# Norm roots and spreads one or two tiles sooner, and two projection pieces between a head's loads and the head

## The chip, the cores and the metric

The kernel runs on one core of one Trainium2 chip. The metric is the device time of one execution in microseconds (us): the median of several runs. A profile is one execution recorded by the hardware profiler.

## The reference

The program is a two-layer backbone over 512 latent tokens and 256 context tokens, model width 1024, all in float32. In each layer, with the same weights for both kinds of token:

- a half-step feed-forward block: the input is normalised by its root mean square, scaled and shifted by a condition ("modulated"), multiplied up to two times 2816 columns, gated with silu, multiplied down, and added to the stream;
- one mixing step: norm and modulation again, one projection to queries, keys and values, split into group A (8 heads, 2-D neighbourhood attention) and group B (8 heads, windowed attention with shared keys, rotary angles and a sink), then an output projection;
- a second half-step feed-forward block.

The norm is what the change is about:

```python
def rms_norm(x, g):
    xf = x.astype(jnp.float32)
    y = xf * lax.rsqrt(jnp.mean(xf * xf, axis=-1, keepdims=True) + NORM_EPS)
    return (y * g.astype(jnp.float32)).astype(x.dtype)

def modulate(h, shift, scale):
    return h * (1 + scale) + shift
```

In the second layer the context has no queries and no second feed-forward block. The output is the latent stream.

## The kernel before

**Numbers and layout.** Activations are kept transposed: 128 partitions by 8 slices d of the model width by 768 token columns (512 latent, 256 context). Every matrix product is done as three products of split operands: each float32 operand becomes a high part (cast on ACT) and a low part (difference on DVE), and PE adds high x high, high x low and low x high (lines 559 to 561 and 930 to 932). The activations' parts are `xh` and `xl`; the weights' are `whi` and `wlo`, made 512 columns at a time by `halves` (148 and 149).

**Token streams.** Most stages run over three streams of 256 columns, `THIRDS`: latent first half, latent second half, context. The last stage of a block goes stream by stream: for each, its tiles of the down projection (or of the output projection, `out_final`), a residual on DVE (807), a square on ACT (475) and a sum of squares on DVE (476). When a stream's tiles are done, `background` starts the next norm of that stream as a Python generator, which moves on by one step with each later call of `tick`.

**The norm as a background job.** `norm` waits `root - 1` ticks, then issues `rstd`: products with a column of ones on PE (505), a scale on DVE (507) and the power -1/2 on POOL (508). At tick `spread` it issues the transposes on PE that spread the result over all partitions into a PSUM bank (514), and then, for eight slices d, the modulation: a multiplication on DVE (520), `xh` on ACT (524), `xl` on DVE (525). Each slice from the third on is to be issued behind the `xl` of two slices earlier. The products of `rstd` and the transposes are to be issued behind the last product traced so far. The pairs (root, spread) come from one table, by kind and stream:

```python
TICKS = {"ffn": [(3, 6), (3, 6), (5, 8)], "mix": [(3, 6), (3, 4), (2, 3)], "lat": [(2, 3), (3, 6)]}
```

"ffn" is a norm in front of a feed-forward block with three streams (twice in the program), "mix" one in front of the mixing step (twice), "lat" one in front of the last block, with two streams (once). `tick` is called after each tile of the last stage, after each two slices in the plain products of the next feed-forward block, and after each piece of the projection. So tick 6 of the first stream falls in the third stream's tiles. The first norm of the program, at its start, doesn't use the table.

**The mixing step.** The projection is cut into nine units of 256 columns (`UNITS`), each into pieces of 128 tokens: 24 products on PE, then a copy to `raw` on ACT (942, two buffers), squares, a reduction, the root on POOL, and for group B the rotation on DVE (960 to 973); the rows go to a scratch in DRAM by SP's queue (981 to 986). The units of group B come first; from then on a piece has a single PSUM bank, tag "mm". Then come 16 heads, B first. `head` loads a pair's query rows (`load_pair`, 1026), values (`load_v`) and keys (`load_k`, through `load_keys`, 994) from the scratch, transposes them on PE (1010) and splits them (1034, 1035, 1070, 1071); `qn` and `kn`, which the loads fill, have one buffer each. `scores` multiplies (1148, 1149). Between the heads `fill` places the other pieces, and then the output projection, by shares of their total.

**Who sets the order.** The program order gives priorities; the order on each engine is fixed when the program is built, by a scheduler that has its own clock (`schedule_with_timeline_sim=True`). An instruction that the scheduler holds ready can go ahead of one that is traced before it. `issue_after` adds an order on one engine that the scheduler must keep. On the chip each engine then runs its own list in order.

Of the kernel before, what the change touches and what calls it, by code (L numbers as in the profile page):

```python
# [10 lines left out]
F32 = mybir.dt.float32  # L11
# [6 lines left out]
P = 128  # L18
D = 1024
KD = 8  # L20
S = 512
C = 256
T = S + C
# [19 lines left out]
SQ, SK, SV = 0, 1024, 2304  # L43
# [123 lines left out]

TICKS = {"ffn": [(3, 6), (3, 6), (5, 8)], "mix": [(3, 6), (3, 4), (2, 3)], "lat": [(2, 3), (3, 6)]}  # L170

FULL = [(0, 0, S), (1, S, T)]
LAT = [(0, 0, S)]
# [4 lines left out]
class Kern:  # L178
# [132 lines left out]
    def background(self, then, i, n, b, s0, s1):  # L311

        kind = "lat" if n == 2 else "mix" if then[1] == 1 else "ffn"
        self.bg.append((self.norm(*then, b, s0, s1, *TICKS[kind][i]), s0))

# [496 lines left out]
    def mixing(self, l, last):  # L812
        nc, ws = self.nc, self.ws
        base = self.at["in", l]
        streams = LAT if last else FULL
        n = streams[-1][2]
        with ExitStack() as c2:
            self.pp = self.open(c2, "ps_m", space=bass.MemoryType.PSUM, reuse_waits="tile")
            self.fp = self.ap = self.open(c2, "mix", reuse_waits="tile")
            self.banks = ("t", TB)  # L820
            self.x = self.ap.tile([P, KD, T], F32, tag="x", name="x")
            self.next_slot, self.wide = 0, -1
            self.jobs, self.held, self.free = [], [], False
            ws.after(base)
            pieces = [(u, t) for u in range(9) for t in range(4 if (last and UNITS[u][0][0] == "q") else 6)]

            def piece():
                u, t = pieces.pop(0)
                if t == 0:
                    self.unit = ws.get(base + u)  # L830
                    ws.after(base + u + 1)
                self.flush(t * P)
                self.project(l, u, t)
                self.tick()
                if not pieces:

                    self.free = True
                    for f in self.held:
                        f()
                    self.held = []  # L840

            with ExitStack() as c3:
                self.rp = self.open(c3, "rope", reuse_waits="tile")
                self.rope_tables(l)
                self.early = True
                while pieces and UNITS[pieces[0][0]][0][-1] == "B":
                    piece()
                self.early = False
            bp = self.open(c2, "bias", reuse_waits="tile")

            self.bias = bp.tile([P, 7, 256], F32, name="bias")
            self.bmask = bp.tile([P, 896], F32, name="bmask")
            nc.sync.dma_start(self.bmask, self.a["bmask"])
            nc.gpsimd.memset(self.bias[:, 3], 0.0)
            outs = [(u, d, z) for u in range(4) for d in (2 * u, 2 * u + 1) for z in streams]

            def out():
                u, d, (b, s0, s1) = outs.pop(0)
                if d % 2 == 0 and s0 == 0:
                    i = self.at["out", l] + u  # L860
                    self.wout = ws.get(i)
                    ws.after(i + 1)
                self.out_b(l, self.wout, d, b, s0, s1)

            cost = lambda: 1.0 if pieces else (outs[0][2][2] - outs[0][2][1]) / S
            total = len(pieces) + sum((z[2][2] - z[2][1]) / S for z in outs)
            state = [0.0]

            def fill(share):
                while (pieces or outs) and state[0] < total * share:  # L870
                    state[0] += cost()
                    piece() if pieces else out()

            nj = 2 if last else 3
            order = list(range(8, 16)) + list(range(8))
            nxt = None
            for i, hh in enumerate(order):
                loaded = nxt or self.head(l, last, hh)
                for j in range(nj):
                    if j == nj - 1 and i < 15:  # L880
                        h2 = order[i + 1]
                        if h2 % 4 == 0 and h2 < 8:

                            while pieces and UNITS[pieces[0][0]][1] % 512 <= 64 * h2:
                                state[0] += 1.0
                                piece()
                        nxt = self.head(l, last, h2)
                    self.push(self.scores(l, hh % 8, hh < 8, ((0, 1), (2, 3), (4, 5))[j], loaded))
                    n = i * nj + j
                    fill((n + 1 + LEAD) / (16 * nj))  # L890
            while self.jobs:
                self.values(*self.jobs.pop(0))
            fill(2.0)
# [118 lines left out]

    def load_pair(self, l, last, pair, A):

        nc, ap, scr = self.nc, self.ap, self.scr
        nq = S if last else T
        qn = ap.tile([P, 6, P], F32, tag="qn", name="qn", bufs=1)
        cs = slice(SQ + pair * P, SQ + pair * P + P)
        if A:
            lat = scr[0:S, cs].rearrange("(r w) c -> r w c", w=64)  # L1020
            for t in range(4):
                nc.sync.dma_start(qn[:, t, :], lat[:, t * 16:t * 16 + 16, :])
            if not last:
                nc.sync.dma_start(qn[:, 4:6], scr[S:T, cs].rearrange("(t p) c -> p t c", p=P))
        else:
            nc.sync.dma_start(qn[:, :nq // P], scr[:nq, cs].rearrange("(t p) c -> p t c", p=P))
        q = [ap.tile([P, T], F32R, tag=f"q{e}", name=f"q{e}", bufs=QB) for e in range(2)]
        for ts in ((0, 1, 2, 3), (4, 5))[:1 if last else 2]:
            src = self.transposed([qn[:, t, :] for t in ts])
            cols = slice(ts[0] * P, ts[-1] * P + P)  # L1030
            for e in range(2):
                own, oth = (slice(0, 64), slice(64, 128)) if e == 0 else (slice(64, 128), slice(0, 64))
                sc = self.gq8[own, l, 0:1] if A else 1.0
                nc.scalar.activation(out=q[e][own, cols], in_=src[own], func=AF.Copy, scale=sc)
                nc.vector.scalar_tensor_tensor(out=q[e][oth, cols], in0=src[own], scalar=sc,
                                               in1=q[e][own, cols].bitcast(F32), op0=ALU.mult, op1=ALU.subtract)
        return q

    def load_v(self, pair, A):

# [17 lines left out]
    def load_k(self, l, A, head, kcol):  # L1058

        nc, ap = self.nc, self.ap  # L1060
        kn = ap.tile([P, 6, P], F32, tag="kn", name="kn", bufs=1)
        self.load_keys(kn, kcol, P, A)
        order = VSLOT if A else range(6)
        kh = ap.tile([P, T], F32R, tag="kh", name="kh", bufs=KB)
        kl = ap.tile([P, T], F32R, tag="kl", name="kl", bufs=KB)
        sc = self.gcol[:, l, 1:2] if A else 1.0
        for ts in ((0, 1, 2, 3), (4, 5)):
            src = self.transposed([kn[:, order[t]] for t in ts])
            cols = slice(ts[0] * P, ts[-1] * P + P)
            nc.scalar.activation(out=kh[:, cols], in_=src, func=AF.Copy, scale=sc)  # L1070
            nc.vector.scalar_tensor_tensor(out=kl[:, cols], in0=src, scalar=sc, in1=kh[:, cols].bitcast(F32),
                                           op0=ALU.mult, op1=ALU.subtract)
        return kh, kl

    def block(self, b, A, head):

# [263 lines left out]
```

## Time and profile before

| what | value |
|---|---|
| median of the runs | 2666.98 us (2657.66 to 2667.18) |
| the profiled execution | 2666.63 us |
| its span, first to last instruction | 2664.5 us |
| mean granted clock of TensorE | 0.992 |
| PE busy | 2589.8 us, 97% |
| DVE busy | 2087.8 us, 78% |
| ACT busy | 1284.1 us, 48% |
| POOL busy | 142.0 us, 5% |

PE is the engine for matrix products, PEld its weight loads, DVE the vector engine, ACT the scalar engine, POOL GpSimd, SP the queue that issues the transfers. A line such as "PE mm L932 <- DVE xl L525: 6.1, 5, 2.0" means that PE stood idle in front of products of line 932 until DVE had written `xl` on line 525, for 6.1 us in all, in 5 places, the longest 2.0 us. A row of a timeline has the start and the length in us, the engine, the line, the operation, out<-in, the shape, the count, and in brackets the idle time in front and what ended it. Names with numbers are merged, so `b`, `t`, `mm` and `sc` are PSUM banks, `st` the small tile of the roots (and, on the lines 935 to 986, a row buffer), `x` a slice of the stream.

### The profile page before, as it was taken

The numbers are of one execution on the slowest core, as the hardware profiler recorded it, in microseconds if no ns is written. First come the engines' busy times: TensorE is split into PE (matmuls) and PEld (weight loads), VectorE is DVE, ScalarE is ACT, GpSimd is POOL, SyncE is SP. The second block draws the span as 40 slices with busy tenths as digits, with TensorE's granted clock in tenths as the row PEclk, the third lists the DMA queues.
The fourth block names the chain that finished last, engine by engine and source line by source line (L and its number), as shares of the span: only waits on it lengthen the run. The fifth ranks groups of instructions, "written<-read, shape, count | busy, mean of one in ns | idle before, by whom it ended". The sixth has DMA issues, their size and how long they took to land. (4 is left out here: it accounts for less than half of the span.)

```text
span 2664.5 us, 47447 instructions
## 1 busy us (share of the span) xinstructions
PE 2589.8 (97%) x17186; PEld 2462.1 (92%) x17186; DVE 2087.8 (78%) x4190; ACT 1284.1 (48%) x2666; POOL 142.0 (5%) x231
## 2 busy tenths in 40 slices
PE   7999999989999999999999999999988999899999
PEld 5999999989999899999999999999988998899998
DVE  7998898677889788777776887686766778777776
ACT  6343343445777653343334533432444677554543
POOL 0000000024111000000000000000003111000000
PEclk9999999999999999999999999999999999999999
DMA  8666647335235536455444366466344336355553
GB/s 321 223 206 204 221 157 223 114 119 152 88 100 163 175 92 214 140 176 185 145 156 133 112 222 211 141 217 209 105 149 135 103 107 183 96 175 166 165 163 116
DMA packets 305866, 431.66 MB, mean 162 GB/s; under 512 B 31408, under 2 KB 177200, under 8 KB 304304
## 3 DMA queue, kind: packets, MB, share of 16 engines
q1 hardware_dynamic: 305632, 428.64, 51.2%
q8 instruction: 135, 2.21, 0.3%
q14 instruction: 99, 0.81, 0.1%
HBM read 343.33 MB, written 88.34 MB: 162 GB/s over the span
## 5 line engine op out<-in xcount | busy, mean ns | idle before, releaser
L148 ACT CAST whi<-wraw 128x512 fp32r<-128x512 f32 (+1 forms) x632 | 381.6, 609 | 698.7 <-PE b L560 595.5
L149 DVE TENSOR_TENSOR wlo<-wraw,whi 128x512 fp32r<-128x512 f32 (+1 forms) x632 | 417.2, 673 | 65.6 <-ACT whi L148 46.1
L561 PE MATMUL b<-xh,wlo 128*128 128x384 f32 (+2 forms) x1472 | 453.9, 313 | 2.6 <-DVE wlo L149 2.6
L560 PE MATMUL b<-hl,whi 128*128 128x512 f32 (+1 forms) x1292 | 432.6, 337 | 0.0
L560 PE MATMUL b<-xl,whi 128*128 128x384 f32 (+2 forms) x1344 | 423.4, 316 | 6.8 <-DVE xl L525 6.6
L561 PE MATMUL b<-hh,wlo 128*128 128x512 f32 (+1 forms) x1292 | 428.8, 336 | 0.0
L559 PE MATMUL b<-xh,whi 128*128 128x384 f32 (+2 forms) x1344 | 418.2, 316 | 2.9 <-ACT xh L524 2.0
L559 PE MATMUL b<-hh,whi 128*128 128x512 f32 (+1 forms) x1292 | 414.5, 337 | 0.0
L560 PE MATMUL b<-x,whi 128*128 128x384 f32 (+1 forms) x1216 | 390.8, 322 | 0.0
L559 PE MATMUL b<-sh,whi 128*128 128x384 f32 (+1 forms) x1216 | 389.8, 323 | 0.4
L561 PE MATMUL b<-sh,wlo 128*128 128x384 f32 (+1 forms) x1216 | 384.0, 322 | 0.5 <-DVE wlo L149 0.5
L461 DVE CUSTOM_DVE_ANT_0 junk<-adaw,sc,bada 128x1024 bf16<-128x1024 f32 x224 | 286.5, 1279 | 15.8 <-DMA adaw<-in_w_ada 15.2
L561 PEld LDWEIGHTS b<-xh,wlo 128*128 128x128 f32 x1472 | 277.0, 189 | 7.5 <-DVE wlo L149 4.3
L148 ACT CAST whi<-wt 128x512 fp32r<-128x512 f32 x228 | 141.8, 622 | 272.6 <-PE b L560 246.7
L560 PEld LDWEIGHTS b<-hl,whi 128*128 128x128 f32 x1292 | 244.7, 189 | 24.9
L561 PEld LDWEIGHTS b<-hh,wlo 128*128 128x128 f32 x1292 | 244.3, 189 | 25.0
L560 PEld LDWEIGHTS b<-xl,whi 128*128 128x128 f32 x1344 | 254.3, 189 | 12.1 <-DVE xl L525 8.1
L559 PEld LDWEIGHTS b<-hh,whi 128*128 128x128 f32 x1292 | 241.1, 189 | 26.0
L559 PEld LDWEIGHTS b<-xh,whi 128*128 128x128 f32 x1344 | 251.8, 189 | 7.3 <-ACT xh L524 2.4
L932 PE MATMUL mm<-whi,xl 128*128 128x256 f32 x800 | 227.9, 287 | 12.1 <-DVE xl L525 12.1
L930 PE MATMUL mm<-whi,xh 128*128 128x256 f32 x800 | 232.1, 292 | 5.2 <-ACT raw L942 4.9
L559 PEld LDWEIGHTS b<-sh,whi 128*128 128x128 f32 x1216 | 228.7, 188 | 3.6 <-ACT whi L148 2.2
(166 smaller groups left out, 4982.9 us busy)
## 6 DMA issues: line engine op xcount, KB each, us to landing
wraw<-in_w_up SPq DMA_DIRECT2D x352, 256.0 KB
adaw<-in_w_ada SPq DMA_DIRECT2D x129, 512.0 KB
wraw<-in_w_down SPq DMA_DIRECT2D x160, 256.0 KB
xsp<-x SPq DMA_DIRECT2D x140, 256.0 KB
xsp<-x SPq DMA_DIRECT2D x184, 128.0 KB
xl<-xsp SPq DMA_DIRECT2D x80, 256.0 KB
xh<-xsp SPq DMA_DIRECT2D x80, 256.0 KB
wraw<-in_w_in SPq DMA_DIRECT2D x72, 256.0 KB
```

What stands on the lines that cost most here:

```text
L148: k.nc.scalar.copy(hi[:, :w], raw[:, :w])
L149: k.nc.vector.tensor_tensor(out=lo[:, :w], in0=raw[:, :w], in1=hi[:, :w].bitcast(F32), op=ALU.subtract)
L461: nc.vector.tensor_tensor_reduce(out=junk, in0=w, in1=self.sc[:, cond, :], scale=1.0, scalar=self.bada[:, l, n:n + 1], op0=ALU.mult, op1=A ...
L559: mm(o, wh, h, start=first, stop=False, skip_group_check=more)
L560: mm(o, wh, l, start=False, stop=False, skip_group_check=more)
L561: self.product = mm(o, wl, h, start=False, stop=last, skip_group_check=more)
L930: nc.tensor.matmul(o, self.xh[:, k, ts], wh, start=k == 0, stop=False)
L932: self.product = nc.tensor.matmul(o, self.xl[:, k, ts], wh, start=False, stop=k == KD - 1)
```

## The change

Three things:

- In `TICKS`, the first two streams of "ffn" and "mix" get the root at tick 2 and the spread at tick 4; the third stream of "mix" gets them at ticks 1 and 2. "lat" and the third stream of "ffn" stay.
- The loads of query rows and of keys are taken out of `load_pair` and `load_k` into functions of their own, `rows_of` and `keys_of`, which first look in the list `asked`.
- In `mixing`, ahead of the heads, the loads of the first head (pair 4 and the keys at SK + 1024) are put into `asked`, and two pieces of the projection are traced behind them; the first head then takes the two tiles from the list. The two pieces are counted in `state`, so `fill` places two fewer behind the first scores.

```diff
--- before.py
+++ after.py
@@ -167,7 +167,7 @@
 
 
 
-TICKS = {"ffn": [(3, 6), (3, 6), (5, 8)], "mix": [(3, 6), (3, 4), (2, 3)], "lat": [(2, 3), (3, 6)]}
+TICKS = {"ffn": [(2, 4), (2, 4), (5, 8)], "mix": [(2, 4), (2, 4), (1, 2)], "lat": [(2, 3), (3, 6)]}
 
 FULL = [(0, 0, S), (1, S, T)]
 LAT = [(0, 0, S)]
@@ -820,7 +820,7 @@
             self.banks = ("t", TB)
             self.x = self.ap.tile([P, KD, T], F32, tag="x", name="x")
             self.next_slot, self.wide = 0, -1
-            self.jobs, self.held, self.free = [], [], False
+            self.jobs, self.held, self.free, self.asked = [], [], False, []
             ws.after(base)
             pieces = [(u, t) for u in range(9) for t in range(4 if (last and UNITS[u][0][0] == "q") else 6)]
 
@@ -873,6 +873,12 @@
 
             nj = 2 if last else 3
             order = list(range(8, 16)) + list(range(8))
+
+            asked = [self.rows_of(l, last, 4, False), self.keys_of(False, SK + 1024)]
+            self.asked = asked
+            for _ in range(2):
+                state[0] += 1.0
+                piece()
             nxt = None
             for i, hh in enumerate(order):
                 loaded = nxt or self.head(l, last, hh)
@@ -1012,18 +1018,8 @@
 
     def load_pair(self, l, last, pair, A):
 
-        nc, ap, scr = self.nc, self.ap, self.scr
-        nq = S if last else T
-        qn = ap.tile([P, 6, P], F32, tag="qn", name="qn", bufs=1)
-        cs = slice(SQ + pair * P, SQ + pair * P + P)
-        if A:
-            lat = scr[0:S, cs].rearrange("(r w) c -> r w c", w=64)
-            for t in range(4):
-                nc.sync.dma_start(qn[:, t, :], lat[:, t * 16:t * 16 + 16, :])
-            if not last:
-                nc.sync.dma_start(qn[:, 4:6], scr[S:T, cs].rearrange("(t p) c -> p t c", p=P))
-        else:
-            nc.sync.dma_start(qn[:, :nq // P], scr[:nq, cs].rearrange("(t p) c -> p t c", p=P))
+        nc, ap = self.nc, self.ap
+        qn = self.rows_of(l, last, pair, A)
         q = [ap.tile([P, T], F32R, tag=f"q{e}", name=f"q{e}", bufs=QB) for e in range(2)]
         for ts in ((0, 1, 2, 3), (4, 5))[:1 if last else 2]:
             src = self.transposed([qn[:, t, :] for t in ts])
@@ -1035,6 +1031,24 @@
                 nc.vector.scalar_tensor_tensor(out=q[e][oth, cols], in0=src[own], scalar=sc,
                                                in1=q[e][own, cols].bitcast(F32), op0=ALU.mult, op1=ALU.subtract)
         return q
+
+    def rows_of(self, l, last, pair, A):
+
+        if self.asked:
+            return self.asked.pop(0)
+        nc, scr = self.nc, self.scr
+        nq = S if last else T
+        qn = self.ap.tile([P, 6, P], F32, tag="qn", name="qn", bufs=1)
+        cs = slice(SQ + pair * P, SQ + pair * P + P)
+        if A:
+            lat = scr[0:S, cs].rearrange("(r w) c -> r w c", w=64)
+            for t in range(4):
+                nc.sync.dma_start(qn[:, t, :], lat[:, t * 16:t * 16 + 16, :])
+            if not last:
+                nc.sync.dma_start(qn[:, 4:6], scr[S:T, cs].rearrange("(t p) c -> p t c", p=P))
+        else:
+            nc.sync.dma_start(qn[:, :nq // P], scr[:nq, cs].rearrange("(t p) c -> p t c", p=P))
+        return qn
 
     def load_v(self, pair, A):
 
@@ -1058,8 +1072,7 @@
     def load_k(self, l, A, head, kcol):
 
         nc, ap = self.nc, self.ap
-        kn = ap.tile([P, 6, P], F32, tag="kn", name="kn", bufs=1)
-        self.load_keys(kn, kcol, P, A)
+        kn = self.keys_of(A, kcol)
         order = VSLOT if A else range(6)
         kh = ap.tile([P, T], F32R, tag="kh", name="kh", bufs=KB)
         kl = ap.tile([P, T], F32R, tag="kl", name="kl", bufs=KB)
@@ -1071,6 +1084,14 @@
             nc.vector.scalar_tensor_tensor(out=kl[:, cols], in0=src, scalar=sc, in1=kh[:, cols].bitcast(F32),
                                            op0=ALU.mult, op1=ALU.subtract)
         return kh, kl
+
+    def keys_of(self, A, kcol):
+
+        if self.asked:
+            return self.asked.pop(0)
+        kn = self.ap.tile([P, 6, P], F32, tag="kn", name="kn", bufs=1)
+        self.load_keys(kn, kcol, P, A)
+        return kn
 
     def block(self, b, A, head):
```

## The prediction

> **What bounds the kernel now.** I read the page's engine line first, then PE's waits over the whole span, then the same view around each norm, then the stretches. The columns of a wait: total us, times, longest us.
>
> ```profile
> span 2664.5 us, 47447 instructions
> ...
> PE 2589.8 (97%) x17186; PEld 2462.1 (92%) x17186; DVE 2087.8 (78%) x4190; ACT 1284.1 (48%) x2666; POOL 142.0 (5%) x231
> ...
> PE b L505 <- DVE acc L476: 13.8, 2, 12.7
> PE mm L932 <- DVE xl L525: 12.1, 10, 2.0
> PE b L514 <- POOL st L508: 6.7, 4, 2.4
> PE b L560 <- DVE xl L525: 6.6, 5, 2.6
> ```
>
> PE is idle for 2664.5 - 2589.8 = 74.7 us, so this is all that any reordering can win, apart from clock. 12.7 us of it is the first norm, at the start, which doesn't use the table of ticks. Around the four norms that do, and at the first head of the first layer (window 600 to 640), the view says:
>
> ```profile
> PE mm L932 <- DVE xl L525: 6.1, 5, 2.0
> PE b L514 <- POOL st L508: 1.2, 1, 1.2
> ...
> PE b L560 <- DVE xl L525: 3.5, 3, 1.7
> ...
> PE b L560 <- DVE xl L525: 2.6, 1, 2.6
> PE b L559 <- ACT xh L524: 0.7, 1, 0.7
> ...
> PE mm L932 <- DVE xl L525: 6.0, 5, 1.7
> PE b L514 <- POOL st L508: 1.2, 1, 1.2
> ...
> PE sc L1148 <- DVE q L1035: 2.1, 1, 2.1
> PE mm L930 <- ACT raw L942: 0.5, 1, 0.5
> PE sc L1149 <- DVE kl L1071: 0.4, 1, 0.4
> ```
>
> Two "mix" norms (near 557 and 1986) cost 7.3 and 7.2 us, two "ffn" norms (near 947 and 1466) 3.5 and 3.3: 21.3 us. PE waits for xl, the last product of the modulation on DVE. The stretches show why it is late (us long, busy us of PE, PEld, DVE, ACT, POOL; granted clock):
>
> ```profile
> 548.30:552.70 4.40, 4.40 (x39) 4.40 (x39) 2.71 (x6) 2.38 (x5) 0.00 (x0) 1.00 0.28 86
> ...
> 557.40:568.50 11.10, 5.07 (x25) 3.81 (x25) 11.10 (x27) 5.72 (x13) 4.06 (x6) 0.80 0.36 114
> 564.00:574.30 10.30, 7.63 (x33) 7.18 (x34) 6.95 (x16) 3.56 (x7) 3.23 (x6) 0.50 0.00 0
> ...
> 938.10:942.50 4.40, 4.40 (x40) 4.40 (x39) 2.63 (x7) 2.29 (x5) 0.69 (x1) 1.00 0.30 99
> 942.50:951.70 9.20, 5.65 (x44) 5.04 (x42) 9.20 (x23) 4.57 (x10) 0.87 (x1) 1.00 0.65 191
> ...
> 1456.00:1460.40 4.40, 4.40 (x40) 4.40 (x39) 2.70 (x6) 2.37 (x5) 0.00 (x0) 1.00 0.18 60
> ...
> 1464.00:1474.00 10.00, 6.71 (x44) 6.31 (x44) 10.00 (x24) 6.03 (x14) 0.87 (x1) 0.83 0.64 184
> ...
> 1976.70:1981.10 4.40, 4.40 (x39) 4.40 (x38) 2.67 (x6) 2.34 (x5) 0.00 (x0) 1.00 0.24 79
> ```
>
> The reader is to see two things. While PE waits, DVE is busy without a break (11.10 of 11.10, 9.20 of 9.20): here DVE is the limit, not the pow on POOL or the transposes. And in the 4.4 us just ahead of each spread DVE is idle for 4.40 - 2.71 = 1.69, 1.77, 1.70 and 1.73 us. That is what an earlier spread can use. Behind the waits the granted clock falls to half.
>
> **The change part by part.** No instruction is added or removed: the same roots, pows, transposes, modulations, loads and pieces stand in another order. The profiled execution took 2666.63 us, 2.1 us more than its span and 0.35 below the median of the runs (2666.98), so the sum against it is a sum against the median too.
>
> *First norm of three (mix and ffn): root 3 to 2, spread 6 to 4.* The first mix norm on PE, and the work its root needs:
>
> ```profile
> 541.72 0.42 DVE L476 TENSOR_TENSOR acc<-acc,g 128x256 f32<-128x256 f32 x1 [0.54 <-ACT g L475]
> ...
> 545.90 0.50 PE L505 MATMUL b<-ones,acc 128*128 128x1 f32 x4
> ...
> 551.73 0.38 PE L514 MATMUL b<-ident,st 128*128 128x128 f32 x2
> ...
> 553.76 0.50 PE L505 MATMUL b<-ones,acc 128*128 128x1 f32 x4
> ...
> 557.38 0.43 PE L514 MATMUL b<-ident,st 128*128 128x128 f32 x2 [1.23 <-POOL st L508]
> ```
>
> 545.90 to 551.73 is three tiles, so a tile of PE is some 1.8 us with its share of the root. The root goes to about 544.1; its sums of squares end at 542.14, so PE doesn't stop for them. The spread goes to about 548.1. The 16 modulating operations of DVE for that norm can then start 3.6 us sooner, but into an engine that has 1.7 us free. One operation takes 0.4 us in a row (three in 1.26 us, below), so four of the 16 are done early. The rest meets the same crowd: weight splits, residuals, sums of squares, and the second norm.
>
> ```profile
> 559.41 1.26 DVE L520 SCALAR_TENSOR_TENSOR x<-x,amul,b 128x256 f32<-128x256 f32 x3
> ...
> 568.02 0.87 DVE L525 SCALAR_TENSOR_TENSOR xl<-x,mod,xh 128x256 fp32r<-128x256 f32 x2
> ...
> 568.55 0.58 PE L932 MATMUL mm<-whi,xl 128*128 128x256 f32 x1 [1.16 <-DVE xl L525]
> ```
>
> The last xl that the first piece needs is the eighth of its norm, yet by 568.5 thirteen have started (two before 557.4, eleven after):
>
> ```profile
> 552.70:557.40 4.70, 0.95 (x2) 1.00 0.66 185
> 557.40:568.50 11.10, 5.27 (x11) 0.80 0.36 114
> ```
>
> So some five belong to the second norm, with as many multiplications in front: about 4 us of DVE that stood ahead of urgent work. With four operations done early up to four of these fall behind the urgent ones (1.6 us); but the second spread also comes 1.2 us sooner, as its wait shrinks, and its operations press in sooner. Bounds for one mix norm: a gain of 7.3 (all waits go) and a loss of 1.6 (four more operations of the second norm ahead of the first). I take the row of idle time, 1.7, and half of the reordering, 0.8: 2.5 each, **-5.0** for two.
>
> For an ffn norm the same 1.7 us is there. But the second spread, so far at tick 6, inside the first products of the next stage, comes at tick 4, ahead of that stage's weight splits, which are traced later; so here interleaving is new. Bounds: gain 3.5, loss 16 x 0.4 = 6.4 (all of the second norm ahead of the first products). I take 1.7 less two operations, 0.8: 0.9, nearest to the idle rows: **-1.8** for two.
>
> *Second norm: root 3 to 2; in mix the spread stays at 4.* The 1.23 us in front of the spread goes (1.8 us more lead, against a wait of 1.23). It stands in a stretch where DVE is the limit, so what is late next is xl: zero of its own, bounds -1.2 to 0 each. In ffn the spread follows its root by two tiles instead of three; the last latency from root to pow's end was 553.76 to 557.33:
>
> ```profile
> 556.46 0.87 POOL L508 TENSOR_TENSOR st<-st,nhalf 128x2 f32<-128x2 f32 x1 [9.02 <-DVE st L507]
> ```
>
> 3.6 us, against two tiles: a wait of 0 to 1.2 can appear, with the first products queued behind the transposes on PE. I take +0.4 each, **+0.8**.
>
> *Third norm in mix: (2,3) to (1,2).* One piece sooner, in front of pieces that need it two pieces later; nothing waited for it. Its pow may stand behind the four rope-table operations on POOL. Zero, bounds 0 to +1.2 each.
>
> *Two pieces behind the loads of the first head.* The loads (one of rows, one of keys, on SP) and the pieces are the same, and the later fills do two pieces fewer, so work is only moved. On SP the two loads stand ahead of the two pieces' stores, which wait for DVE in any case. The buffers of rows and keys are single, so the next pair's load, queued on SP behind the transposes, comes up to two pieces later; it is needed two heads on, and costs nothing until then. First layer: the wait of 2.1 us for q (the row above) stands behind a DVE with the rope's backlog; two pieces later that backlog is smaller. I take **-2.0**, bounds -3.0 (q and the 0.5 and 0.4 behind it) to +1. Second layer:
>
> ```profile
> 2039.83 0.38 PE L930 MATMUL mm<-whi,xh 128*128 128x256 f32 x1 [2.80 <-ACT raw L942]
> ...
> 2042.67 0.38 SPq L1026 DMA_DIRECT2D qn<-scr  x1
> ...
> 2043.74 0.37 ACT L942 COPY raw<-mm 128x256 f32<-128x256 f32 x1 [2.62 <-DVE t L970]
> ...
> 2045.57 0.48 DVE L970 TENSOR_TENSOR t<-raw,rt 128x128 f32<-128x128 f32 x2
> ...
> 2046.35 1.11 PE L1010 MATMUL t<-ident,qn 128*128 128x128 f32 x4 [3.53 <-DMA qn<-scr]
> ```
>
> One piece already runs at 2039.83, ahead of the transposes, whose load, issued at 2042.67, ends PE's wait at 2046.35. A second one needs the single "mm" bank, so ACT's raw copy, so a free raw buffer (two exist), so DVE's rope work, which reaches 2046.05: the 3.53 us wait only changes its name. **0**, bounds -3.5 to +3.5.
>
> *Clock.* 564.00:574.30 ran at 0.50: 33 products took 7.63 us of PE, 0.23 each, against 0.113 in 548.30:552.70 (39 in 4.40). So a fall costs the 24 products of a piece 24 x 0.117 = 2.8 us. In the Trainium skill, "TensorE: Matmul & The Clock Gate", section "HAM oscillation — how this bites in real kernels", the clock falls for gaps of PE above about 3.4 us. The trace disagrees: the longest of the five waits around this fall is 2.0 us, and it is their sum that counts. By that rule shorter waits win no clock, and the sum would be 1.7 us less. I take one fall of the three at the norms (two mix, one ffn) avoided, the weakest (1464:1474 at 0.83: 0.17 x 10 = 1.7 us): **-1.7**; bounds -1.7 - 2 x 2.8 = -7.3 and, for one more fall, +2.8.
>
> Sum: -5.0 - 1.8 + 0.8 - 2.0 - 1.7 = -9.7; 2666.6 - 9.7 = **2657**, or -0.36%. The measurement tells a change from none at about 0.5%, 13.3 us; this is inside.
>
> **Rivals.** *All norm waits go.* If the earlier spread lets the first norm's 16 operations run before the crowd (the build may order DVE so, since they are traced sooner), 21.3 us go, with 7.3 of clock and 2.0 at the head: 2636. For it: the start is 3.6 us sooner and 16 operations are only 6.4 us. Against it: DVE has 1.7 free, and its total is unchanged. A half-way case, 14 to 20 gained, is counted here.
>
> *Nothing that counts moves.* If DVE is the limit in the strict sense, and the idle 1.7 us get filled by operations that nobody waits for, the waits only change names: xl becomes weight splits, q becomes a raw copy. 2666, give or take 3. For it: DVE's unbroken rows.
>
> *Slower: the second norm in front.* At the ffn norms its 16 operations stand ahead of the splits that the first products need. Four the early start pays; each beyond costs PE 0.4: 12 x 0.4 = 4.8 each, 9.6 for two. With the mix norms at their losing bound (3.2), two more falls of the clock (5.6), the term of 0.8 and the 2.0 of the head: 9.6 + 3.2 + 5.6 + 0.8 - 2.0 = +17.2, 2684. It passes 13.3 from about 10 of the 16 at each. For it: the order of tracing. Against it: the second norm's own chain through ACT leaves gaps that splits fill.
>
> **How the numbers follow.** Forecast 0.46 (gain 3 to 14); all waits go, or more than half of them, 0.34; nothing moves 0.10; slower 0.10. A tail of 0.02 of the forecast lies beyond 13.3. So faster 0.34 + 0.02 = 0.36, same 0.44 + 0.10 = 0.54, slower 0.10. The range goes down to 2640, into the first rival, and up to 2671, past the second (2669) and past no gain with one more fall of the clock (2669); about 0.1 is left out on each side. The forecast's own range is 2653 to 2664.
>
> **What would show it.** Right: the spreads near 548, 938, 1456 and 1977; the 1.7 us idle in front filled; DVE still without a break in the stretch behind; xl waits of 4 to 5 us in place of 6 for a mix norm; no L514 wait in mix; q's wait at the first head under 1; the 3.5 us at the second layer's head still there, under this or another name. Wrong: xl waits gone and the clock at 1.00 through both mix norms (then DVE's order, not its total, was the limit), or new waits for wlo at the ffn norms.

## The result and the profile after

The changed kernel took 2647.66 us (median; 2642.75 to 2651.07) against 2666.98 for the kernel before: 19.3 us less, a ratio of 0.9932 with a 95% interval of 0.9919 to 0.9946. That is 0.7% faster, outside the half per cent that tells a change from none. The forecast was 2657, in a range from 2640 to 2671, and called no change, as it lay inside that half per cent. So the range held the time, and the likeliest case did not. What came is the half-way case that the prediction counted to its first rival, a gain of 14 to 20. Of the executions behind the experiments, one of e4 (10190 us) and one of the kernel before beside it (14525 us) are far outliers, which the ratios leave out and the medians hardly feel.

The profiled execution took 2651.06 us, near the top of its runs, so it shows a gain of 15.6, not 19.3. In it the granted clock was 0.50 from 2264.0 to 2270.8 us, far from the places of the change, where the kernel before had 1.00 at the same products; PE was busy for 5.80 us of that, and half of it, some 3 us, is an estimate of the cost. From the page and PE's waits over the whole span (us in all, times, longest):

```profile
span 2649.3 us, 47426 instructions
...
PE 2588.2 (98%) x17186; PEld 2461.7 (93%) x17186; DVE 2085.4 (79%) x4190; ACT 1283.2 (48%) x2666; POOL 150.6 (6%) x231
...
PE mm L938 <- DVE xl L525: 8.4, 6, 2.0
PE b L514 <- POOL st L508: 6.8, 5, 2.4
```

Lines behind the table have moved: the pieces' products are L936 to L938 (930 to 932 before), the raw copy L948 (942), the transposes L1016 (1010), the scores L1169 and L1170 (1148, 1149). PE's idle time fell from 74.7 us to 61.1. The xl wait of the pieces went from 12.1 to 8.4 us, and the one of 6.6 us in front of L560 is all but gone. Now the same places as before the change, in the order mix, ffn, ffn, mix:

```profile
PE mm L938 <- DVE xl L525: 4.0, 3, 1.9
...
PE b L514 <- POOL st L508: 1.5, 2, 1.2
...
PE b L514 <- POOL st L508: 1.2, 1, 1.2
...
PE mm L938 <- DVE xl L525: 4.4, 3, 2.0
```

The 7.3 and 7.2 us of the mix norms are 4.0 and 4.4; the 3.5 and 3.3 of the ffn norms are 1.5 and 1.2, and there xl isn't waited for at all. The first heads of the two layers, in the changed kernel: first layer, then second. The last two rows are the second layer's in the kernel before. (`kl` is the low part of the keys; `stat` holds a head's running extremes and sums, which DVE makes from the scores.)

```profile
PE mm L937 <- DVE wlo L149: 1.0, 2, 0.6
PE sc L1169 <- DVE stat L1174: 1.0, 1, 1.0
PE sc L1170 <- DVE kl L1084: 0.8, 1, 0.8
PE sc L1169 <- DVE q L1031: 0.4, 1, 0.4
...
PE mm L936 <- ACT raw L948: 2.7, 4, 1.1
PE t L1016 <- DMA qn<-scr: 1.6, 1, 1.6
...
PE mm L930 <- ACT raw L942: 4.1, 3, 2.8
PE t L1010 <- DMA qn<-scr: 3.5, 1, 3.5
```

The PE instructions stand in the same number (17186) in every kernel here, so the n-th product can be compared with the n-th product. The table takes the start of a product in each profiled execution, less its start in the kernel before, and gives how much that difference changes over each place, in us (negative: time won). The places are products 2990 to 3420, 6100 to 6400, 9200 to 9560, 12150 to 12540 and 12700 to 12950; "rest" is all other stretches together, and shows how much two executions differ where little or nothing is changed.

| kernel | mix norm 1 | ffn norm 1 | ffn norm 2 | mix norm 2 | second layer's head | rest |
|---|---|---|---|---|---|---|
| after | -5.0 | -1.9 | -3.0 | -3.1 | -6.0 | +3.8 |
| e1 ticks only | -3.8 | -2.4 | -3.0 | -1.9 | -5.8 | -0.7 |
| e2 pieces only | -1.3 | +0.4 | +1.7 | +5.3 | -2.8 | -3.8 |
| e3 mix ticks only | -3.8 | +2.5 | +2.1 | +3.0 | -6.2 | +0.3 |
| e4 first norm only | -7.2 | -3.0 | -4.6 | -6.3 | -1.0 | +1.7 |
| e12 e3, other bank | -4.7 | +1.9 | +1.8 | -3.4 | -5.2 | +3.1 |

One figure of this table can be off by 2 to 3 us, and the clock does it. e3 and e8 (below) have the same instruction lists up to the second layer's mixing step. At the second ffn norm both wait 0.67 us for xh and 2.62 us for xl; behind that e3's clock falls and e8's doesn't, and e8 stands at -0.6 there where e3 stands at +2.1. First e3, then e8:

```profile
1465.00:1475.00 10.00, 7.69 (x43) 7.69 (x43) 9.69 (x24) 5.71 (x12) 0.54 (x1) 0.66 0.46 141
...
1462.00:1472.00 10.00, 7.51 (x63) 7.49 (x64) 10.00 (x25) 5.66 (x12) 0.76 (x1) 1.00 0.47 149
```

So the norms are read below from several kernels. e5, e9, e10 and e11, which have e4's first pair and the second stream's mix spread a tile later than the change, give much the same as e4: -6.7 to -7.0, -2.8 to -3.1, -4.3 to -5.2 and -5.7 to -6.8 at the four norms.

### The profile page after: what moved, and what is told of

Read it like the earlier page. It is cut to its first block, busy times and chain, and to the rows that moved or that the text cites. A ratio compares the mean times of both kernels' runs of the same rounds, so it can differ in the third digit from the quotient of the medians.

```text
span 2649.3 us, 47426 instructions
## 1 busy us (share of the span) xinstructions
PE 2588.2 (98%) x17186; PEld 2461.7 (93%) x17186; DVE 2085.4 (79%) x4190; ACT 1283.2 (48%) x2666; POOL 150.6 (6%) x231
## 5 line engine op out<-in xcount | busy, mean ns | idle before, releaser
L560 PE MATMUL b<-hl,whi 128*128 128x512 f32 (+1 forms) x1292 | 432.6, 337 | 0.0
L560 PE MATMUL b<-xl,whi 128*128 128x384 f32 (+2 forms) x1344 | 423.2, 316 | 0.6 <-DVE xl L525 0.5
L560 PE MATMUL b<-x,whi 128*128 128x384 f32 (+1 forms) x1216 | 390.8, 322 | 0.0
L560 PEld LDWEIGHTS b<-hl,whi 128*128 128x128 f32 x1292 | 244.7, 189 | 24.9
L560 PEld LDWEIGHTS b<-xl,whi 128*128 128x128 f32 x1344 | 254.8, 190 | 5.2 <-DVE xl L525 1.1
L938 PE MATMUL mm<-whi,xl 128*128 128x256 f32 x800 | 225.9, 284 | 8.4 <-DVE xl L525 8.4
L936 PE MATMUL mm<-whi,xh 128*128 128x256 f32 x800 | 229.7, 290 | 3.6 <-ACT raw L948 3.1
```

Of the source, the lines that this page charges most:

```text
L560: mm(o, wh, l, start=False, stop=False, skip_group_check=more)
L936: nc.tensor.matmul(o, self.xh[:, k, ts], wh, start=k == 0, stop=False)
L938: self.product = nc.tensor.matmul(o, self.xl[:, k, ts], wh, start=False, stop=k == KD - 1)
```

## The experiments

All medians and ratios, each against the kernel before on the same chip (2664.86 us for e1 to e4, 2666.77 for e5 to e8, 2665.51 for e9 to e12). PSUM is the memory that PE's products are written to; it has several banks, and each stage of the kernel opens a pool of its own over the same banks. The bank columns are read from the programs as built: the PSUM bank of the second norm's spread at the second mix norm, and the banks of the first two pieces behind it. The last two columns are PE's waits from the profiles: for L520 there, and for raw and qn together at the second layer's first head.

| kernel | mix pairs | spread's bank; pieces' banks | median us | ratio, interval | L520 wait | raw + qn |
|---|---|---|---|---|---|---|
| before | (3,6) (3,4) (2,3) | 2; 0, 1 | 2666.98 | | none | 7.6 |
| after | (2,4) (2,4) (1,2) | 2; 0, 4 | 2647.66 | 0.9932, 0.9919 to 0.9946 | none | 4.3 |
| e1 | (2,4) (2,4) (1,2) | 4; 0, 4 | 2650.91 | 0.9949, 0.9937 to 0.9961 | 2.3 | 3.7 |
| e2 | (3,6) (3,4) (2,3) | 0; 0, 1 | 2671.25 | 1.0026, 1.0016 to 1.0036 | 12.8 | 7.0 |
| e3 | (2,4) (2,4) (1,2) | 0; 0, 4 | 2661.19 | 0.9984, 0.9973 to 0.9994 | 12.1 | 4.3 |
| e4 | (2,4) (3,4) (2,3) | 7; 0, 1 | 2646.25 | 0.9924, 0.9911 to 0.9937 | none | 6.5 |
| e5 | (2,4) (3,5) (2,3) | 1; 0, 4 | 2642.93 | 0.9916, 0.9903 to 0.9928 | none | 7.0 |
| e6 | (1,3) (3,4) (2,3) | 0; 0, 1 | 2653.75 | 0.9953, 0.9941 to 0.9965 | 8.1 | 6.5 |
| e7 | (2,4) (3,4) (1,2) | 7; 0, 4 | 2643.65 | 0.9918, 0.9905 to 0.9931 | none | 3.7 |
| e8 | (2,4) (2,4) (1,2) | 0; 0, 4 | 2662.36 | 0.9986, 0.9977 to 0.9995 | 12.0 | 3.1 |
| e9 | (2,4) (3,5) (1,2) | 1; 0, 3 | 2644.07 | 0.9919, 0.9905 to 0.9932 | none | 6.5 |
| e10 | (2,4) (3,5) (1,2) | 1; 0, 3 | 2645.14 | 0.9924, 0.9911 to 0.9938 | none | 6.8 |
| e11 | (2,4) (3,5) (1,3) | 1; 0, 3 | 2641.42 | 0.9910, 0.9897 to 0.9924 | none | 7.2 |
| e12 | (2,4) (2,4) (1,2) | 0; 1, 5 | 2654.33 | 0.9960, 0.9947 to 0.9972 | none | 2.4 |

### Which part: e1, e2, e3

e1 is the kernel before with the new table and without the moved pieces; e2 is the changed kernel with the old table; e3 is the kernel before with the three new mix pairs alone.

```diff
-TICKS = {"ffn": [(3, 6), (3, 6), (5, 8)], "mix": [(3, 6), (3, 4), (2, 3)], "lat": ...}
+TICKS = {"ffn": [(2, 4), (2, 4), (5, 8)], "mix": [(2, 4), (2, 4), (1, 2)], "lat": ...}   # e1
+TICKS = {"ffn": [(3, 6), (3, 6), (5, 8)], "mix": [(2, 4), (2, 4), (1, 2)], "lat": ...}   # e3
```

> The kernel before with the new table of ticks alone; the pieces and loads of the first head stay as before. In the traces of before and after, counted by the n-th product of PE, the changed kernel gained 4.8 and 3.6 us at the two mix norms, 1.5 and 3.0 at the two ffn norms, and about 6 us at the first head of the second layer. Theory A (the two moved pieces make the 6 us): this run has 2667 - 13 = 2654 us, and at the second layer's first head the waits of 2.8 us for the raw copy and 3.5 us for qn are still there. Theory B (the 6 us come from the ticks, since DVE enters the projection with less behind it): 2648, and those waits are shortened to about 1 and 1.6 us here too.

> The changed kernel with the old table of ticks: only the loads of the first head and the two pieces are moved. Theory A (the pieces make the gain at the second layer's head): 2661 us, with qn's wait about 1.6 us. Theory B (the ticks make it): 2666, with waits of 3.5 us for qn and 2.8 us for the raw copy as before. Both: the xl waits at the four norms as before (6.1, 3.5, 2.6, 6.0 us), and the first layer's head within 1 us of before.

> The kernel before with the new ticks for mix alone. If the steps of the trace add: 2667 - 4.8 - 3.6 = 2658.6 us by theory A, 2653 by theory B (the second layer's head gains 6 us with it); the ffn norms keep their xl waits of 3.5 and 2.6 us.

The table of ticks carries the gain: the intervals of e1 and of the whole change overlap. It also has the 6 us at the second layer's first head, which the moved pieces were thought to stand for; its waits there (3.7 us) are as short as after's, while e2, which has the pieces, keeps 7.0. (e2's time there fell by 2.8 us all the same, which is the size by which one figure can be off.) e2 is slower than before, and e3 gains almost nothing though it holds half of the table; both their times lie above what either theory gave. Both lose it in one place. The rows are PE's waits in e3, e2 and e1 at the second mix norm:

```profile
PE mm L930 <- DVE x L520: 12.1, 1, 12.1
...
PE mm L936 <- DVE x L520: 12.8, 1, 12.8
...
PE mm L930 <- DVE x L520: 2.3, 1, 2.3
```

A product of the projection doesn't read x. What it can share with L520 is the PSUM bank that L520 reads, the spread's. In e3 the wait begins behind the second spread and ends behind the last of the two norms' sixteen L520:

```profile
1984.31 0.38 PE L514 MATMUL b<-ident,st 128*128 128x128 f32 x2
1996.77 0.55 PE L930 MATMUL mm<-whi,xh 128*128 128x256 f32 x1 [12.08 <-DVE x L520]
...
1996.16 0.47 DVE L520 SCALAR_TENSOR_TENSOR x<-x,amul,b 128x256 f32<-128x256 f32 x1
```

### The first norm alone: e4

```diff
+TICKS = {"ffn": [(2, 4), (3, 6), (5, 8)], "mix": [(2, 4), (3, 4), (2, 3)], "lat": ...}
```

> The kernel before with root 2 and spread 4 for the first stream alone, in ffn and mix; second and third streams as before. Theory (DVE's idle time in front of the first spread, 1.7 us each, and operations of the second norm falling behind carry the gain; the wait in front of the second spread stands under DVE's cover): the xl waits fall as in the changed kernel, to 4.0 to 4.4 us at mix and under 1 us at ffn, and the ffn norms have no wait on line 514; 2667 - 8 to 13 = 2654 to 2659. Rival (the second norm's lead of two ticks in mix carries it, by taking the 1.2 us wait away): waits of 1.2 us on line 514 stay and the gain is under 4 us, 2663 or more.

e4 is as fast as the whole change, and better than it at each of the four norms (-21.1 us together against -13.0); it lacks only the second layer's head. Its gain, 18.6 us over the kernel before beside it, is more than its theory gave (8 to 13). At the ffn norms e4 differs from e1 in the second stream's pair alone, and there moving that pair cost time: e1 has -2.4 and -3.0 and the whole change -1.9 and -3.0, while the seven kernels that leave it and move the first (e4 to e7, e9 to e11) have -2.7 to -3.1 and -4.3 to -5.2. At the mix norms the third pair differs too, and no run here moves the second without it. The waits at the two mix norms:

```profile
PE mm L932 <- DVE xl L525: 2.0, 2, 1.3
PE b L514 <- POOL st L508: 1.8, 2, 1.3
...
PE mm L932 <- DVE xl L525: 2.0, 2, 1.3
PE b L514 <- POOL st L508: 1.3, 1, 1.3
```

The L514 wait, which the change removes, stays, and the xl wait is half of after's 4.0 and 4.4.

### The bank: e6, e8, e12

e6 moves the first pair one tile further, (1, 3) in ffn and mix on top of e4. e8 and e12 are e3 with the banks of the second layer's pieces shifted, e8 by the turn of the rotation, e12 by a tile asked for and left unused.

```diff
+            self.turn += last              # e8, in mixing
+            if last:                       # e12, at the same place
+                self.mm_bank()
```

> The edit: before with the first stream at (1, 3) in ffn and mix; the rest as before. Theory A (each tile of lead is worth what DVE idles in a tile, some 0.85 us, and the first norm's operations are not held up): the xl wait of 2.0 us left at the mix norms in e4 goes and the run ends 1 to 4 us under e4, 2642 to 2645. Rival B (the root comes before its sums of squares are there): a wait of 0.5 to 2 us in front of L505 for acc of L476 appears at each of the four norms, and takes back all of the gain; 2646 to 2652. Rival C (DVE cannot take more ahead): waits as in e4 within 0.5 us each and the time within 2 of it.

> The edit: e3 (all three mix pairs new, ffn as before, no moved pieces), with the rotation of the PSUM banks advanced by one place at the start of the second layer's projection, so that the first piece there takes another bank than the one the second norm's spread holds. Theory A (the 12.1 us wait of the first piece of the second layer for L520 is a bank that is in use): the wait is gone, PE's steps at the mix norm near 1986 are as in after (3 to 5 us sooner than before, in place of 3.8 later), and the run ends at 2649 to 2655, 7 to 10 under e3. Rival B (DVE's order is at fault, L520 of the second norm simply runs late and something else would wait for it): the wait stays at 8 us or more under the same or another name, and the run ends within 3 of 2661.

> The edit: e3 (all three mix pairs new, ffn as before, no moved pieces), with a PSUM tile of the projection asked for and left unused ahead of the first piece of the second layer. In the program as built, the second norm's spread of that layer stands in bank 0 in e3 and in e8 alike, and so does the first piece; here the first piece stands in bank 1, and a piece two later is the first in bank 0. Theory A (the 12 us wait is that bank): the first piece no longer waits for L520 and begins some 10 us sooner; at most 6 us of the wait come back at the later piece; the xl waits of 4 to 5 us, which the 12 us covered, are seen again, and the run ends at 2650 to 2658, 3 to 10 under e3. Rival B (the operations on DVE are late, whatever the bank): PE stands still for 10 to 12 us behind the second spread under this or another name, and the run ends at 2660 to 2664.

e8 missed: the wait stayed at 12.0 us, because the turn changes the piece's tag but the first tile of the newly opened pool is placed in bank 0 under either tag. Read alone it spoke for the rival. e12 moved the piece to bank 1, and the wait is gone; PE goes from the second spread straight into the piece, and what was behind it is seen instead:

```profile
1983.16 0.38 PE L514 MATMUL b<-ident,st 128*128 128x128 f32 x2
1983.30 0.37 PE L932 MATMUL mm<-whi,xh 128*128 128x256 f32 x1
...
PE mm L934 <- DVE xl L525: 4.8, 3, 2.3
```

The time fell by some 7 us (2661.19 to 2654.33; ratios 0.9984 and 0.9960, intervals apart), as theory A of e12 put it. All kernels agree with it: e2, e3, e6 and e8, where spread and first piece share bank 0, wait 8 to 13 us; e1, where the second piece has the spread's bank 4, waits 2.3; the nine others don't wait. The ticks and the pieces far from this place only changed which bank the spread drew: e1 and e3 differ in ffn pairs alone.

e6 ran into this too. Its time, 2653.75, lies above all three of its cases for this reason. At the other norms it gained little over e4 (-8.1, -2.7 and -4.3 us in the terms of the table of places, against -7.2, -3.0 and -4.6): the waits for L505 that its rival B named came (0.6 and 0.5 us, at the ffn norms only), and at the mix norms the xl wait went and the L514 wait grew to 2.4.

### The second and third norm: e5, e7, e9, e11

All four are e4 with other mix pairs for the second and third stream (the table above has them).

> The edit: before with the first stream at (2, 4) in ffn and mix, as in e4, and in mix the second stream at (3, 5) in place of (3, 4). Theory A (what counts is that the second norm's operations stay behind the first's on DVE): a second spread one tile later still takes fewer DVE slots ahead of the first norm's last xl, so at the mix norms the xl wait of 2.0 us and the L514 wait of 1.8 us (as in e4) shrink to 2 us together or less, no new wait comes, and the run ends at 2641 to 2645, 0 to 4 us under e4. Rival B (DVE's sum of work is the limit, not its order): the L514 wait goes and comes back as an xl wait; the sum at each mix norm stays within 1 us of e4's, and the run at 2646 within 2. Rival C (the second norm becomes the late one): its tiles are wanted by the projection's pieces for the second stream, so a new xl wait of 1 to 4 us stands in front of the seventh and eighth piece, and the run ends at 2648 to 2652.

> The edit: before with the first stream at (2, 4) in ffn and mix, as in e4, and the third stream of mix at (1, 2) in place of (2, 3). Theory A (the third mix norm's earlier tick makes the gain of some 6 us at the second layer's first head, which e1 and e3 have and e4 has not): the raw and qn waits around 2010 to 2060 fall as in e1, and the run ends at 2640 to 2643. Rival B (that gain comes from the second mix norm at (2, 4), not from the third): the second layer's head stays as in e4, with a raw wait of 3 us and a qn wait of 2, and the run ends at 2645 to 2648. Rival C (the third norm's operations now press into the first norm's modulation): the xl waits at the mix norms grow by 1 to 3 us each, and the run ends at 2648 to 2652.

> The edit: before with the first stream at (2, 4) in ffn and mix, the second stream of mix at (3, 5) as in e5, and its third at (1, 2) as in e7; no moved pieces. Theory A (the two gains over e4 are separate: L514 waits of the second norm, 3.3 us in the medians, and the second layer's first head, 2.6): the run ends at 2638 to 2642, 5 to 8 under e4, with no L514 wait for the second spread, one of 2 to 3 us for the third at each mix norm, and raw and qn waits at 2010 to 2060 of 4 us together or less. Rival B (a second spread one piece in and a third spread two pieces in stand so close that the third waits longer or its operations press into the second's): xl or L514 waits at each mix norm grow by 2 us or more against e7, and the run ends at 2644 to 2650.

> The edit: before with the first stream at (2, 4) in ffn and mix, the second stream of mix at (3, 5), the third at (1, 3): its root one piece sooner than before, its spread where it was. Theory A (the spread's place makes the gain at the second layer's first head, since the third norm's 16 operations on DVE come a piece sooner): the head stays as in e5, with raw waits of 4 to 5 us and a qn wait of 2, and the run ends at 2641 to 2645, as e5. Rival B (an earlier root is enough): the raw waits there fall to 2 or less, no L514 wait stands ahead of the third spread, and the run ends at 2636 to 2640, under e9.

Their medians lie from 2641.4 to 2644.1, and their intervals overlap with each other and with e4's; none is shown to be faster than another. In the traces, e5 puts the second norm a tile later: the L514 wait goes, the xl wait is 2.6 and 2.7 us in place of 2.0, one of 0.5 for L507 comes at the first mix norm, and the sums there fall from 3.8 to 3.1 and from 3.3 to 2.7: in part the wait only changed its name. e7 moves the third pair alone on top of e4. It has short waits at the second layer's head and wins 5.9 us there, where e4 wins 1.0. But the third spread now waits at the mix norms, 3.1 and 3.2 us longest, and e7 stands at -3.5 and -4.4 there, where e4 stands at -7.2 and -6.3: in the traces the gain is paid back. The xl waits are e4's.

```profile
PE b L514 <- POOL st L508: 4.4, 2, 3.1
...
PE b L514 <- POOL st L508: 4.5, 2, 3.2
...
PE t L1010 <- DMA qn<-scr: 2.1, 1, 2.1
PE mm L930 <- ACT raw L942: 1.6, 4, 0.5
```

e9 was to have both gains and doesn't: raw and qn are 4.3 and 2.2 us again. Over all kernels these two waits are 2.4 to 4.3 us where the third mix pair is (1, 2) and the second spread stands at tick 4, and 6.5 to 7.6 in every other one. That pairing is what the runs show; how a spread of the third stream, some 40 us ahead of the head, shortens its raw wait was not followed to the end. e11 has the lowest median of all, 2641.42, and its interval lies just within reach of after's (up to 0.9924 against from 0.9919); they were not run beside each other. In e11's profile 2.8 us of the lead over e5 were won from 2255 to 2275 us, where the code of the two kernels is the same: the granted clock was 1.00 there in e11 and 0.83 in e5.

### The pieces by themselves: e10

e10 is e9 with the early loads and the two moved pieces of the change.

> The edit: e9 with the two moved pieces of the change (its loads of the first head asked for early as well); it differs from e9 in the moved pieces alone. Theory A (the pieces are worth nothing): q's wait of 1 to 2 us at the first layer's first head goes and comes back as raw waits of the moved pieces; PE reaches the products behind both heads within 1 us of e9, and the run ends within 2 of e9. Rival B (the prediction's term): 2.0 us are gained at the first layer's head, none at the second's, and the run ends 2 us under e9, 1 to 3. Rival C (the moved pieces cost): the second layer's head gets a raw wait of 2 to 4 us ahead of the first moved piece, and the run ends 1 to 4 over e9.

2645.14 against 2644.07: no difference that counts. First the first layer's head, then the second's, in e9 and behind them in e10:

```profile
PE sc L1148 <- DVE q L1035: 2.2, 1, 2.2
PE sc L1148 <- DVE stat L1153: 0.6, 1, 0.6
...
PE mm L930 <- ACT raw L942: 4.3, 3, 3.0
PE t L1010 <- DMA qn<-scr: 2.2, 1, 2.2
...
PE sc L1169 <- DVE stat L1174: 1.5, 1, 1.5
PE sc L1170 <- DVE kl L1084: 0.8, 1, 0.8
PE sc L1169 <- DVE q L1031: 0.6, 1, 0.6
...
PE mm L936 <- ACT raw L948: 5.9, 3, 4.4
PE t L1016 <- DMA qn<-scr: 0.9, 1, 0.9
```

q's wait falls by 1.6, and stat and kl, both from DVE as well, take 1.3 of it. Over products 3580 to 3760, which hold the first layer's head, e10 won 1.2 us over e9 and e2 1.0 over before, while the change lost 0.2 against e1. At the second head the wait for the load falls by 1.3 and the one for raw grows by 1.6.

## Why the prediction was right, and where it was not

**What bounds it.** Right: PE waits for DVE's xl behind the norms, and the first spreads came at 547.58, 935.18, 1450.79 and 1968.01, where they were forecast less what the kernel had won until there. Three small readings in the working are off and decide nothing: a tile with its share of the root is 5.83 / 3 = 1.94 us (1.78 without); a modulating operation took 0.47 us, not 0.4; and the slower rival passes 13.3 us from about 11 of the 16 operations, not 10.

**First mix norm, -2.5 each: mis-sized, 4.4 and 4.5.** The stretch from the place on PE where the new spread stands to the last xl wait of the first piece, in before and then after; in each, all engines, then L520 alone, then L525 alone on DVE:

```profile
548.13:568.55 20.42, 13.12 (x94) 11.65 (x92) 18.56 (x44) 11.70 (x25) 4.93 (x7) 0.89 0.41 123
548.13:568.55 20.42, 6.36 (x14) 0.89 0.41 123
548.13:568.55 20.42, 6.27 (x13) 0.89 0.41 123
...
547.58:563.60 16.02, 12.03 (x93) 11.13 (x91) 15.82 (x39) 10.31 (x23) 1.68 (x1) 0.91 0.61 163
547.58:563.60 16.02, 5.58 (x12) 0.91 0.61 163
547.58:563.60 16.02, 4.61 (x10) 0.91 0.61 163
```

It is 4.4 us shorter. DVE's idle time in it went from 20.42 - 18.56 = 1.86 to 0.20: 1.7 won, the term of idle time to the digit. The other 2.7 are work that no longer stands ahead of the last xl. 2.4 of it are modulating operations, 22 in place of 27; eight operations L525 of the first norm are needed, so five of the second norm stood ahead in before, as the prediction had counted, and two in after. The term "half of the reordering, 0.8" is the step that failed: it measured 2.4, above its own bound of 1.6. An earlier start let DVE's list put urgent work ahead of work that could wait, and that was worth more than the idle time. At the second mix norm the same stretch went from 20.84 to 16.32 us. In e4, where the second spread comes 9.3 us behind the first in place of 7.9, it is shorter again by 1.3 us, with ten L520 and nine L525. The third norm's root comes behind the stretch in both, so these 1.3 us are the second pair's. The clock adds to it: in e4 it stays at 1.00 through the first mix norm and is 0.61 for 4.3 us behind the second; in the change it is 0.50 for 6.8 and for 10.2 us.

```profile
546.21:560.95 14.74, 11.44 (x93) 10.83 (x92) 14.54 (x36) 9.44 (x21) 0.87 (x1) 1.00 0.55 172
```

**Ffn norms, -0.9 + 0.4 each: mis-sized.** -1.9 and -3.0 in the trace. The wait of 0 to 1.2 in front of L514 came, at 1.2, above the 0.4 taken; but xl's 3.5 and 2.6 us went altogether. No new wait for the splits of the next stage came. Without the second pair, e4 won 1.1 and 1.6 more at these norms, and the later kernels of its kind agree; the slower rival had put 4.8 on each.

**Second mix spread, "stands under DVE's cover, zero".** The wait of 1.23 went, as forecast, and its removal was worth nothing, or less: e4 keeps it and is better at both mix norms. The slower rival's mechanism, the second norm's operations ahead of urgent ones, was at work here: 1.3 us in the stretch above. The whole difference of after against e4, 2.2 and 3.2 us for a mix norm, holds the clock and the third pair as well and isn't split by any run; in no case is it on the scale that would have turned the sign.

**Third norm, zero; second layer's head, zero: wrong.** They are tied. 6.0 us were won at that head, by the ticks and without the pieces, and e7 shows that the third pair alone, on top of e4, is enough for it. It has a price that the bounds of 0 to +1.2 didn't hold: in e7 the third spread waits for 3.1 and 3.2 us. In the change that wait doesn't show. The wait of 3.5 did not change its name; with raw it went from 7.6 to 4.3, and with it went a fall of the clock. That fall is most of the 6.0: PE was busy for 8.55 of the 10.2 us that ran at 0.50 (2045.5 to 2055.7 in before), and half of it, 4.3 us, is an estimate of its cost. How the third norm acts on this head stays open. The stretch of 20 us around it, before and then after:

```profile
2036.00:2056.00 20.00, 12.87 (x73) 12.02 (x71) 15.12 (x41) 8.27 (x19) 9.87 (x15) 0.74 0.59 163
...
2024.00:2044.00 20.00, 15.61 (x122) 14.33 (x120) 15.29 (x38) 9.87 (x21) 11.50 (x13) 1.00 0.67 193
```

**The two pieces, -2.0 at the first layer: wrong in what it is worth.** q's wait went under 1, as forecast, and the time followed by 1.2 us at most: the scores behind wait for kl and stat of the same DVE.

**Clock, -1.7 for one fall: it came, in part by chance, and one more came.** The ffn stretch that ran at 0.83 runs at 1.00. Of the five kernels with the old ffn pairs, four show this fall and e8 doesn't, with the same waits as e3; of the nine that spread the first ffn norm sooner, none does. So the ticks make the fall rarer, and one profile couldn't have shown it.

```profile
1458.60:1468.60 10.00, 10.00 (x87) 10.00 (x87) 10.00 (x24) 7.66 (x16) 0.00 (x0) 1.00 0.56 160
...
560.80:567.60 6.80, 4.71 (x20) 4.42 (x21) 6.80 (x17) 2.80 (x6) 2.85 (x5) 0.50 0.50 128
```

The second row is the first mix norm after the change, still at half clock, though no wait around it is above 1.9 us; in this it goes against the rule of 3.4 us in the Trainium skill, "TensorE: Matmul & The Clock Gate", section "HAM oscillation — how this bites in real kernels", that the prediction set aside. That the sum of the waits counts in its place, as the prediction had it, isn't shown either: the same waits of 0.67 and 2.62 us ended with a fall in e3 and without one in e8.

**The sum.** -9.7 was forecast, -15.6 measured in the profiled execution and -19.3 in the medians. In the profile the norms gave 13.0 with their clock, where 7.7 had been taken; the second head gave 6.0 more, and the rest together took 3.8 back. In that rest lie the first layer's head, which gave 0.3 where 2.0 had been taken, and the fall at 2264, some 3 us. The rival that nothing moves is refuted, and so is the slower one as a whole. The price that no case had is the bank, and the change escaped it by the luck of its draw: with the same mix pairs, e3 lost 3.0 us at the second mix norm where the change won 3.1.

## What to carry to other kernels

Where an engine is full around a stage boundary, count which of its operations stand ahead of the one that is waited for, not only its idle time: here five operations fewer ahead of it (2.4 us) were worth more than the idle stretch (1.7 us). Moving the urgent norm alone was enough; in the traces, moving the one behind it as well gave part of it back, though the medians of the two kernels can't be told apart. And when a small change of order costs several us somewhere far away, look at which buffer the waiting instruction shares with the one that it waits for, before blaming the order. A figure from one place in one profile can be off by the clock; read it in several kernels that share the code there.

## What the runs showed of the hardware that was not expected

A product that waits for a PSUM bank stops PE completely, though its first operands are there, as e12 shows: in e3 nothing ran on PE for 11.8 us, and the products behind it then ran at about half clock for 6 us more (0.50, then 0.55). The rows are that stretch and the two behind it:

```profile
1984.90:1996.70 11.80, 0.00 (x0) 0.00 (x0) 11.80 (x28) 5.71 (x14) 3.35 (x6) 0.66 0.59 171
1996.70:1998.70 2.00, 1.93 (x9) 1.96 (x10) 0.99 (x2) 0.47 (x1) 0.27 (x1) 0.50 0.03 8
1998.70:2002.70 4.00, 4.00 (x22) 4.00 (x22) 0.00 (x0) 0.00 (x0) 0.00 (x0) 0.55 0.00 0
```

The Trainium skill, "Perfetto Trace Analysis", section "Matmuls", says that independent groups of products should rotate through different PSUM banks, so that one is read while the next is computed. These runs agree, and add that a rotation within each pool does not do it across two pools: the spread's bank belongs to the stage that ends, the piece's to the one that begins.
